# A two-layer attention trunk on one core: the planner takes any two accesses to one PSUM bank, one of them a write, as dependent

## The chip, the cores and the metric

The kernel runs on one core of one Trainium2 chip. The metric is the device time of one execution in microseconds, the median of three runs. All durations further down come from one profiled execution of the kernel before.

## What is computed

Two layers, each a pre-norm mixer over 512 tokens of width 1024. One input projection feeds three causal attention branches; each branch is gated, projected and merged. The change touches the part of branch A, differential attention with four heads of two softmax maps each:

```python
s = jnp.einsum('bqhcd,bkhcd->bhcqk', qb, k) * scale
pr = masked_softmax(s, kpos[None, :] <= tpos[:, None])
a = pr[:, :, 0] - lam * pr[:, :, 1]
o = jnp.einsum('bhqk,bkhe->bqhe', a, v)          # 4 heads, 128 wide
...
o = rmsnorm(o, subln_g) * (1.0 - lam_init)
branches = jnp.stack([o_a * silu(a_g), o_b * silu(b_g), o_c * silu(c_g)], axis=2)
x = x + jnp.sum(sigmoid(merge) * (branches @ w_up), axis=2) @ w_out
```

Around it stand the projections of the other branches, which are computed in three products of split operands (high by high, low by high, high by low), so that TensorE carries three matmuls of 512 columns for each 128 by 128 block of weights.

## The kernel before, in words

The program first records every operation in a `Plan` (`add`, line 272), with the tiles that it reads and writes. `Plan.put_down` (line 387) then goes through the recorded operations with a table of costs and sets, for each of the five engines, the order in which they are written into the program; operations that may run on two engines (weight splits on ACT or POOL, subtractions and sums on POOL or DVE) get their engine there too. Dependences of the reckoning come from `View.box` (line 152), a rectangle of partitions and columns: two accesses depend on each other where their rectangles meet (`meet`, line 329). The program that comes out of it gets its semaphores from the framework below, by what it was told in that order.

In PSUM the program holds two rings of tiles, three of `mm` for the projections and five of `at` for scores, transposes and attention outputs. Each tile is 128 partitions by 512 columns of f32 and is one bank.

`attend_a(h)` (line 1085) is one head of branch A: scores and exponentials of the two maps, the difference of the maps into `P`, and then, as a tail that is woven into other work, `weigh_a` (line 1108). It transposes the four row blocks of `P` into PSUM, copies each to `PTh` on ACT, and multiplies. Products of row block i go to columns 128 i to 128 i + 127 of one bank `po`; block i has i + 1 matmuls, ten for a head. I call the four groups put 0 to put 3. Then ACT reads the bank in four pieces of 128 columns, each divided by its row sum, and squares each piece:

```python
T.matmul(po[:, i * P : (i + 1) * P], at[:, j * P : (j + 1) * P],
         AV[j][:, h * P : (h + 1) * P], start=j == 0, stop=j == i)
...
A.activation(on[:, i * P : (i + 1) * P], po[:, i * P : (i + 1) * P], AF.Copy, scale=rr[:, 0, i : i + 1])
A.activation(junk, on[:, i * P : (i + 1) * P], AF.Square, accum_out=ss[:, i : i + 1])
```

Behind the four reads stand three small DVE instructions and twelve small POOL instructions (an inverse square root, tiles `ss`, `ni`, `rs`, `nt`), four scalings of `on` on ACT, and in `turn` four transposes of `on` on TensorE. In the profile the reads are `o<-at,rr`, the squares `dg<-o`, the scalings `o<-o,rs`, the products `at<-X,PTh`, and the turn's transposes `at<-consts,o`.

Woven around heads 2 and 3 is `c_query` (line 904), which projects a query of branch C, multiplies it by R on DVE into a tile `t`, and lets TensorE multiply that tile by the compressed keys (`at<-KCb,t`), four matmuls. Its softmax has two small DVE instructions, `cm<-cm,gate` and `cm<-cm,consts`, 128 by 8.

Heads 0 to 3 of layer 0 run from about 140 to 262 us of the span, those of layer 1 from about 820 to 945 us. Everything is recorded by one line of the program, so every instruction of the profile has line 471.

Of the kernel before, what the change touches and what calls it, by code (L numbers as in the profile page):

```python
# [126 lines left out]
class View:  # L127
# [23 lines left out]

    def box(self):

        a, b = int(self.cells[(0,) * self.cells.ndim]), int(self.cells[(-1,) * self.cells.ndim])
        w = self.tile.width
        return a // w, b // w, a % w, b % w
# [62 lines left out]
class Plan:  # L219
# [52 lines left out]
    def add(self, names, call, args, kw):  # L272
# [15 lines left out]
        for x in op.ins:  # L288
            box = x.box()
            for b, w in x.tile.writes:  # L290
                if self.meet(b, box):
                    op.after.add(w)
        for x in op.outs:
            box, t = x.box(), x.tile
            for line in (t.writes, t.reads):
                for b, w in line:
                    if self.meet(b, box):
                        op.after.add(w)
# [1231 lines left out]
```

## Time and profile before

| | |
|---|---|
| three runs | 1411.82, 1410.4, 1412.04 us; median 1411.82 |
| the profiled execution | 1409.82 us, its span 1408.0 us |
| mean granted clock of TensorE | 0.996 of full |
| TensorE busy | 1378.9 us, 98% of the span, 6882 matmuls |
| VectorE busy | 1046.4 us, 74% |
| ScalarE busy | 790.3 us, 56% |
| GpSimd busy | 567.3 us, 40% |
| TensorE without work, all gaps | about 29 us |

Busy time of matmuls runs to a modelled end, so successive matmuls overlap by some 0.16 us; what a stop costs is read from start to start. The page's table of slices shows TensorE in its highest tenth all along, and the other engines between.

### The profile page before, as it was taken

The numbers are of one execution on the slowest core, as the hardware profiler recorded it, in microseconds if no ns is written. First come the engines' busy times: TensorE is split into PE (matmuls) and PEld (weight loads), VectorE is DVE, ScalarE is ACT, GpSimd is POOL, SyncE is SP. The second block draws the span as 40 slices with busy tenths as digits, with TensorE's granted clock in tenths as the row PEclk, the third lists the DMA queues.
The fourth block names the chain that finished last, engine by engine and source line by source line (L and its number), as shares of the span: only waits on it lengthen the run. The fifth ranks groups of instructions, "written<-read, shape, count | busy, mean of one in ns | idle before, by whom it ended". The sixth has DMA issues, their size and how long they took to land.

```text
span 1408.0 us, 20777 instructions
## 1 busy us (share of the span) xinstructions
PE 1378.9 (98%) x6882; PEld 1153.3 (82%) x6882; DVE 1046.4 (74%) x2348; ACT 790.3 (56%) x1831; POOL 567.3 (40%) x613
## 2 busy tenths in 40 slices
PE   9999999999999999999999999999999999999997
PEld 7888877888888888888887888778888888888886
DVE  7688888888887566555785888897888855666566
ACT  6455655866764356334444656567677734643443
POOL 3464466545343152122251744774445322313040
PEclk9999999999999999999999999999999999999998
DMA  6223221111222221342422231312112222124221
GB/s 246 98 83 101 72 89 62 61 61 53 75 68 83 85 88 61 106 149 98 147 83 97 83 98 52 106 55 67 60 61 68 76 83 89 62 75 157 97 91 68
DMA packets 67932, 123.65 MB, mean 88 GB/s; under 512 B 7920, under 2 KB 10224, under 8 KB 67824
## 3 DMA queue, kind: packets, MB, share of 16 engines
q1 hardware_dynamic: 62640, 113.14, 24.5%
q10 hardware_dynamic: 5184, 9.18, 1.9%
q8 instruction: 54, 0.88, 0.2%
q14 instruction: 54, 0.44, 0.1%
HBM read 117.57 MB, written 4.72 MB: 87 GB/s over the span
## 4 chain that ended last, share of the span: by engine, by line
PE 89%; DVE 5%; ACT 1%; issue 1%; POOL 0%; DMA 0%; DVEq 0%; POOLq 0%; ACTq 0%; SPq 0%
PE mm L471 70%; PE at L471 19%; DVE t L471 1%; DVE nt L471 0%; DVE P L471 0%; POOL nt L471 0%; DVE cm L471 0%; DMA raw<-W 0%; DVE K L471 0%; DVE rstd L471 0%; ACT o L471 0%; DVE g L471 0%; DVE wlo L471 0%; DVE x L471 0%; DVE hr L471 0%
## 5 line engine op out<-in xcount | busy, mean ns | idle before, releaser
L471 PE MATMUL mm<-HI,whi 128*128 128x512 f32 x1240 | 496.9, 401 | 2.1 <-POOL whi L471 1.1
L471 PE MATMUL mm<-HI,wlo 128*128 128x512 f32 x1240 | 488.7, 394 | 1.6 <-DVE wlo L471 1.0
L471 PE MATMUL mm<-LO,whi 128*128 128x512 f32 x1240 | 488.0, 394 | 1.3 <-DVE LO L471 1.3
L471 POOL TENSOR_SCALAR whi<-raw 128x512 fp32r<-128x512 f32 (+1 forms) x191 | 130.5, 684 | 535.2 <-PE mm L471 357.2
L471 POOL TENSOR_TENSOR wlo<-raw,whi 128x512 fp32r<-128x512 f32 (+1 forms) x191 | 256.9, 1348 | 188.0 <-ACT whi L471 151.6
L471 PEld LDWEIGHTS mm<-HI,wlo 128*128 128x128 f32 x1240 | 233.9, 189 | 51.0 <-DVE wlo L471 1.4
L471 PEld LDWEIGHTS mm<-HI,whi 128*128 128x128 f32 x1240 | 234.3, 189 | 41.8 <-POOL whi L471 1.6
L471 ACT CAST whi<-raw 128x512 fp32r<-128x512 f32 (+1 forms) x205 | 125.2, 614 | 254.8 <-PE mm L471 185.5
L471 PEld LDWEIGHTS mm<-LO,whi 128*128 128x128 f32 x1240 | 234.4, 189 | 40.0 <-DVE LO L471 2.3
L471 DVE TENSOR_TENSOR wlo<-raw,whi 128x512 fp32r<-128x512 f32 (+1 forms) x205 | 149.7, 735 | 79.6 <-ACT whi L471 43.9
L471 ACT ACTIVATE P<-P,mx 128x512 f32<-128x512 f32 (+3 forms) x256 | 142.4, 557 | 65.7 <-DVE mx L471 64.6
L471 PE MATMUL at<-K,Q 128*128 128x256 f32 (+3 forms) x608 | 138.9, 325 | 0.0
L471 PEld LDWEIGHTS at<-K,Q 128*128 128x128 f32 x608 | 103.1, 189 | 16.1 <-issue 0.5
L471 DVE TENSOR_TENSOR t<-mm,R 128x512 f32<-128x512 f32 (+1 forms) x101 | 69.0, 683 | 61.1 <-PE mm L471 57.8
L471 DVE CUSTOM_DVE_ANT_0 P<-at,consts 128x128 f32<-128x128 f32 x208 | 93.8, 470 | 21.6 <-PE at L471 20.5
L471 DVE TENSOR_TENSOR PTl<-at,PTh 128x512 fp32r<-128x512 f32 x192 | 87.0, 484 | 28.2 <-ACT PTh L471 21.6
L471 POOL TENSOR_TENSOR Q<-t,Q 64x512 fp32r<-64x512 f32 x64 | 87.5, 1367 | 34.9 <-ACT Q L471 29.3
L471 PE MATMUL at<-consts,P 128*128 128x128 f32 x560 | 96.1, 272 | 0.8 <-ACT PTh L471 0.7
L471 ACT ACTIVATE P<-P,rc 128x128 f32<-128x128 f32 x192 | 92.0, 552 | 7.9 <-DVE rc L471 6.9
L471 ACT CAST PTh<-at 128x512 fp32r<-128x512 f32 x192 | 74.4, 420 | 38.4 <-PE at L471 31.1
L471 PEld LDWEIGHTS at<-consts,P 128*128 128x128 f32 x560 | 71.5, 140 | 22.1 <-ACT PTh L471 1.3
L471 PE MATMUL mm<-BRh,whi 128*128 128x512 f32 x192 | 77.0, 405 | 0.5 <-DVE t L471 0.5
(222 smaller groups left out, 2126.5 us busy)
## 6 DMA issues: line engine op xcount, KB each, us to landing
raw<-W SPq DMA_DIRECT2D x396, 256.0 KB, 2.6
raw<-WK SPq DMA_DIRECT2D x16, 176.0 KB, 2.3
X<-xT ACTq DMA_DIRECT2D x10, 256.0 KB, 4.1
res<-X ACTq DMA_DIRECT2D x8, 256.0 KB, 2.0
X<-res ACTq DMA_DIRECT2D x8, 256.0 KB, 3.4
out<-K SPq DMA_DIRECT2D x8, 256.0 KB, 2.5
X<-xT SPq DMA_DIRECT2D x6, 256.0 KB, 4.8
P<-xN SPq DMA_DIRECT2D x3, 512.0 KB, 6.0
```

The lines of the kernel that those rows point to most:

```text
L471: getattr(getattr(self.nc, op.engine), call)(*real, **kw)
```

## The change

A view of a PSUM tile now has the whole tile as its rectangle. For the recorded dependences this means: a read of some columns depends on the last write to the bank that was recorded before it, whatever its columns; a write depends on every read and write of that bank recorded before it.

```diff
     def box(self):
 
+        if self.tile.space == "psum":
+            return 0, self.tile.shape[0] - 1, 0, self.tile.width - 1
         a, b = int(self.cells[(0,) * self.cells.ndim]), int(self.cells[(-1,) * self.cells.ndim])
         w = self.tile.width
         return a // w, b // w, a % w, b % w
```

Of the 11,239 recorded operations 24 get an operation to wait for that they had not waited for, directly or through others on the same engine: the first three reads `o<-at,rr` of each of the eight heads (four heads, two layers). They waited for put 0, 1 and 2, and now wait for the last matmul of put 3. All else in the program is the same, but the order of the five engines is worked out anew. It differs from the first of these reads on to shortly behind the fourth head, in either layer; ahead of that, between the layers and behind, the instructions stand as before, and the DMA queue of SP is the same throughout. In the two stretches some 300 of 6673 TensorE instructions, 200 of DVE's, 100 of ACT's and 60 of POOL's stand elsewhere. 22 two-input operations (weight remainders `wlo`, rotary sums) go from POOL to DVE and 16 the other way; ACT gets two casts more than it gives.

The first place is ACT at head 0 of layer 0. `o_420` is the head's output, `at_385` its PSUM bank, `dg` the square; the wait is by semaphore, named after the engine waited for. Before:

```order
L471 ACTIVATE o_420_1657<-at_385_1648,rr_342_1375 128x128 [waits PE_49]
L471 ACTIVATE K_395_1663<-t_393_1641 64x512 [waits DVE_49]
L471 ACTIVATE K_395_1663<-t_393_1641 64x512
L471 ACTIVATE K_397_1678<-t_393_1641 64x512 x2
L471 ACTIVATE dg_421_1689,ss_386_1690<-o_420_1657 128x128 [waits Activation_49]
L471 ACTIVATE o_420_1657<-at_385_1648,rr_342_1375 128x128 [waits PE_49]
L471 ACTIVATE dg_422_1699,ss_386_1690<-o_420_1657 128x128 [waits Activation_49]
L471 ACTIVATE o_420_1657<-at_385_1648,rr_342_1375 128x128
L471 ACTIVATE dg_423_1713,ss_386_1690<-o_420_1657 128x128 [waits Activation_49]
L471 ACTIVATE t_409_1724<-t_408_1715 128x512 [waits DVE_49]
L471 ACTIVATE o_420_1657<-at_385_1648,rr_342_1375 128x128 [waits PE_49]
L471 ACTIVATE dg_424_1737,ss_386_1690<-o_420_1657 128x128 [waits Activation_49]
```

After:

```order
L473 CAST whi_446_1702<-raw_445_1595 128x512 [waits DMAHW1_49,PE_49,Pool_49]
L473 ACTIVATE t_409_1714<-t_408_1706 128x512 [waits DVE_49]
L473 ACTIVATE o_420_1722<-at_385_1648,rr_342_1375 128x128 [waits PE_49]
L473 ACTIVATE dg_421_1729,ss_386_1730<-o_420_1722 128x128 [waits Activation_49]
L473 ACTIVATE o_420_1722<-at_385_1648,rr_342_1375 128x128
L473 ACTIVATE dg_422_1739,ss_386_1730<-o_420_1722 128x128 [waits Activation_49]
L473 ACTIVATE o_420_1722<-at_385_1648,rr_342_1375 128x128
L473 ACTIVATE dg_423_1747,ss_386_1730<-o_420_1722 128x128 [waits Activation_49]
L473 ACTIVATE o_420_1722<-at_385_1648,rr_342_1375 128x128
L473 ACTIVATE dg_424_1769,ss_386_1730<-o_420_1722 128x128 [waits Activation_49]
```

The four reads, which stood between other work and each waited for its put, now stand together behind the casts and the key halves `K`, and only the first of them waits for TensorE.

The second place is TensorE at the same head, between put 0 and put 2 (`X` is a tile of values, `PTh` a transposed block; `mm_405` is a projection that is woven in). Before:

```order
L471 MATMUL mm_405_1628<-LO_32_153,whi_400_1556 128x512
L471 MATMUL mm_405_1628<-HI_31_144,wlo_401_1561 128x512
L471 MATMUL at_385_1648<-X_142_810,PTh_390_1528 128x128
L471 MATMUL at_385_1648<-X_143_819,PTh_390_1528 128x128 [waits Activation_49]
L471 MATMUL mm_405_1628<-HI_33_155,whi_400_1556 128x512
L471 MATMUL mm_405_1628<-LO_34_162,whi_400_1556 128x512
```

After:

```order
L473 MATMUL mm_405_1628<-LO_32_153,whi_400_1556 128x512
L473 MATMUL mm_405_1628<-HI_31_144,wlo_401_1561 128x512
L473 MATMUL at_385_1648<-X_142_810,PTh_390_1528 128x128
L473 MATMUL at_385_1648<-X_143_819,PTh_390_1528 128x128
L473 MATMUL mm_405_1628<-HI_33_155,whi_400_1556 128x512
L473 MATMUL mm_405_1628<-LO_34_162,whi_400_1556 128x512
```

The instructions are the same ones. Before, the second matmul of put 1, which writes columns 128 to 255, waits for ACT, which by then has the read of columns 0 to 127 in its queue; now it waits for nothing.

The third place is DVE ahead of the second `c_query` product of layer 0, whose operand is `t_644`. `mm_638` is its projection, `acc_92` the top-k scores of branch B, `P_549` the difference of the softmax maps of head 3, `cm_601` the factors of the first `c_query`. Before:

```order
L471 TENSOR_TENSOR t_629_2535<-mm_608_2390,R_76_403 128x512 [waits PE_49]
L471 MATCH_REPLACE acc_92_633<-m8_567_2352,acc_92_633 128x384
L471 RECIPROCAL rr_642_2265<-st_618_2455 128x4 [waits Activation_49]
L471 TENSOR_TENSOR cm_601_2444<-cm_601_2444,gate_44_594 128x8 [waits DVE_49]
L471 MAX m8_625_2556<-acc_92_633 128x8
L471 TENSOR_TENSOR cm_601_2444<-cm_601_2444,consts_3_185 128x8 [waits DVE_49]
L471 TENSOR_TENSOR t_644_2570<-mm_638_2503,R_76_403 128x512 [waits PE_49]
L471 STREAM_SHUFFLE t_646_2577<-mm_638_2503 128x512 [waits Pool_49]
```

After:

```order
L473 TENSOR_SCALAR ni_615_2543<-ss_569_2424 128x4 [waits DVE_49]
L473 TENSOR_SCALAR rs_614_2546<-ni_615_2543 128x4 [waits DVE_49]
L473 TENSOR_TENSOR cf_643_2549<-st_550_2163,rr_642_2300 128x4
L473 SCALAR_TENSOR_TENSOR g_631_2555<-t_630_2540,t_629_2532 128x512 [waits Activation_49]
L473 TENSOR_SCALAR cf_643_2549<-cf_643_2549,nlam_90_405 128x4 [waits DVE_49]
L473 SCALAR_TENSOR_TENSOR P_549_2149<-P_617_2469,cf_643_2549,P_549_2149 128x128 [waits DVE_49]
L473 SCALAR_TENSOR_TENSOR P_549_2149<-P_617_2469,cf_643_2549,P_549_2149 128x256
L473 SCALAR_TENSOR_TENSOR P_549_2149<-P_617_2469,cf_643_2549,P_549_2149 128x384
L473 SCALAR_TENSOR_TENSOR P_549_2149<-P_617_2469,cf_643_2549,P_549_2149 128x512
L473 TENSOR_TENSOR t_644_2590<-mm_638_2512,R_76_403 128x512 [waits PE_49]
L473 STREAM_SHUFFLE t_646_2605<-mm_638_2512 128x512
```

The two small `cm_601` instructions, which stood one and three places ahead of `t_644`, now stand seventeen and eighteen places ahead of it. In their place stand the four differences of head 3 and three small instructions of head 2 (`ss`, `ni`, `rs`). On TensorE, the product with `KCb` came six matmuls of 512 columns behind the last of `mm_638`; now three of them and nine transposes of `P_549` stand there.

## Rows read from the trace of the kernel before

**Rows 1.** the page: busy time of each engine, and the chain that ended last

```profile
PE 1378.9 (98%) x6882; PEld 1153.3 (82%) x6882; DVE 1046.4 (74%) x2348; ACT 790.3 (56%) x1831; POOL 567.3 (40%) x613
...
PE 89%; DVE 5%; ACT 1%; issue 1%; POOL 0%; DMA 0%; DVEq 0%; POOLq 0%; ACTq 0%; SPq 0%
```

**Rows 2.** stretches; columns: busy per engine (instructions), granted clock, DMA share, GB/s

```profile
200.00:262.00 62.00, 58.93 (x301) 47.77 (x300) 54.49 (x126) 37.78 (x103) 43.97 (x58) 0.97 0.20 67
...
880.00:945.00 65.00, 61.84 (x327) 50.82 (x327) 57.64 (x141) 39.45 (x110) 48.62 (x69) 1.00 0.27 86
```

**Rows 3.** PE's waits over the span: for whom, us in total, times, longest

```profile
PE at L471 <- ACT o L471: 4.0, 8, 0.6
```

**Rows 4.** timeline, head 0: start, length, engine, operation [idle before <-whom]

```profile
148.52 0.38 PE L471 MATMUL at<-X,PTh 128*128 128x128 f32 x2
...
148.94 0.37 ACT L471 ACTIVATE o<-at,rr 128x128 f32<-128x128 f32 x1 [0.28 <-PE at L471]
...
149.36 0.49 PE L471 MATMUL at<-X,PTh 128*128 128x128 f32 x2 [0.46 <-ACT o L471]
...
153.83 1.05 PE L471 MATMUL at<-X,PTh 128*128 128x128 f32 x8
```

**Rows 5.** timeline, head 2: a short hold, then the last long one

```profile
210.87 0.60 PE L471 MATMUL at<-consts,P 128*128 128x128 f32 x4
...
211.49 0.71 PE L471 MATMUL at<-X,PTh 128*128 128x128 f32 x4
...
905.38 0.71 PE L471 MATMUL at<-X,PTh 128*128 128x128 f32 x4 [0.46 <-ACT o L471]
```

**Rows 6.** timeline: ACT's reads of head 0, its scaling, and head 1's first turn

```profile
152.11 0.34 ACT L471 ACTIVATE o<-at,rr 128x128 f32<-128x128 f32 x1
...
152.79 0.35 ACT L471 ACTIVATE o<-at,rr 128x128 f32<-128x128 f32 x1
...
155.68 0.31 ACT L471 ACTIVATE dg<-o 128x128 f32<-128x128 f32 x1
...
160.64 1.28 ACT L471 ACTIVATE o<-o,rs 128x128 f32<-128x128 f32 x4 [1.20 <-POOL rs L471]
...
189.70 0.33 PE L471 MATMUL at<-consts,o 128*128 128x128 f32 x1 [0.62 <-ACT o L471]
```

**Rows 7.** timeline: ahead of the second product with KCb, both layers

```profile
227.87 2.52 POOL L471 TENSOR_TENSOR wlo<-raw,whi 128x512 fp32r<-128x512 f32 x2
...
228.11 1.09 DVE L471 TENSOR_TENSOR cm<-cm,gate 128x8 f32<-128x8 f32 x1
...
229.72 0.69 DVE L471 TENSOR_TENSOR cm<-cm,consts 128x8 f32<-128x8 f32 x1
...
231.07 1.10 PE L471 MATMUL at<-KCb,t 128*128 128x64 f32 x8 [1.59 <-DVE t L471]
...
922.87 1.10 PE L471 MATMUL at<-KCb,t 128*128 128x64 f32 x8 [1.60 <-DVE t L471]
```

**Rows 8.** tile cm: duration in ns, min/median/max, first and last start

```profile
L471 DVE TENSOR_TENSOR cm<-cm,gate x8: 172/174/1103, 228.1 to 1023.9; 128x8 f32<-128x8 f32 x8
...
L471 DVE TENSOR_TENSOR cm<-cm,consts x8: 166/168/692, 229.7 to 1024.1; 128x8 f32<-128x8 f32 x8
```

**Rows 9.** one stretch right behind 231.07, columns as in rows 2

```profile
232.00:236.00 4.00, 4.00 (x13) 3.14 (x13) 3.90 (x11) 1.67 (x3) 3.56 (x6) 0.57 0.10 37
```

**Rows 10.** timeline of PE: the wait for one weight remainder

```profile
191.96 0.40 PE L471 MATMUL mm<-HI,whi 128*128 128x512 f32 x1
...
192.19 0.40 PE L471 MATMUL mm<-LO,whi 128*128 128x512 f32 x1
...
193.57 0.50 PE L471 MATMUL mm<-HI,wlo 128*128 128x512 f32 x1 [0.98 <-DVE wlo L471]
```

**Rows 11.** tile wlo, 140 to 262 us: duration in ns, min/median/max

```profile
L471 POOL TENSOR_TENSOR wlo<-raw,whi x18: 1264/1292/1742, 141.3 to 258.7; 128x512 fp32r<-128x512 f32 x18
...
L471 DVE TENSOR_TENSOR wlo<-raw,whi x11: 682/685/1121, 143.7 to 240.6; 128x512 fp32r<-128x512 f32 x11
```


## The prediction

> **What bounds the kernel now.** I read the page first: TensorE is busy for 1378.9 of 1408.0 us, and 89% of the chain that ended last is its own work [rows 1]. The change adds and takes away no matmul, so time can only come from where TensorE stops, some 29 us in all, and from its clock. The new order differs from the old one only around the four heads of branch A in either layer, so I looked there next: in the stretch 200 to 262 us TensorE is without work for 3.1 us and DVE is busy for 54.5 of 62, in 880 to 945 us for 57.6 of 65 [rows 2]. TensorE is the bound, and DVE stands close behind it. Then I asked whom TensorE waits for: the longest entry over the whole span is ACT's tile `o`, 8 times, 4.0 us [rows 3]. The timeline shows what that is. In head 0 the first matmul of put 1 starts at 148.52, ACT reads the columns of put 0 from 148.94 to 149.31, and only at 149.36 does TensorE go on with the next matmul, which writes other columns of that bank [rows 4]. Its semaphore names ACT. So on the chip the program already takes the bank as one, and the plan, which did not know it, put the read between two writes.
>
> **What the reads cost now.** Eight matmul passes of put 3 take 1.05 us, of which the last is 0.27 long, so a pass comes every 0.11 us and a matmul, two passes, every 0.22. The held one comes 0.84 us after the one before it, a loss of 0.62 [rows 4]. There are six like it: put 1 of heads 0 and 1, put 3 of head 2, in both layers, the first at 149.36 and the last at 905.38, each with 0.46 us idle [rows 4, 5]. They make 2.8 of the 4.0 us; the other two entries, 0.62 and 0.61, are of another kind, below. Six more are short: four transposes from 210.87 in 0.60 us, the last of them starting about 211.20, and the held matmul at 211.49 where 0.11 later was possible, a loss of 0.18 [rows 5]. That is 6 x 0.62 + 6 x 0.19 = **4.9 us**. In the new order every one of the 24 reads stands behind the last matmul of its put 3, in all eight heads, so all of this goes. Nothing hides it now: TensorE's other work stands behind the held matmul in the same queue. What is late next is ACT's chain to the turn.
>
> **What the later reads cost.** Three reads and three squares that were done early now follow put 3. Back to back, reads come every 0.68 us (152.11, 152.79), so the last square starts about 2.5 us after put 3, and from the last square to the end of the first scaling it is 155.68 to 160.64 + 0.40, or 5.4 [rows 6]. That makes 7.8 us from put 3 to a possible turn, where it was 6.2. In the new order TensorE has 44, 55, 76 and 67 instructions of other work between put 3 and the turn of heads 0 to 3, from start to start, at 0.23 us for a matmul of 512 columns [rows 10], 0.11 for a transpose or a pass [rows 4, 5] and so on, 9.4, 11.4, 15.6 and 12.8 us; before, head 1 had 27 in 5.5 us and waited for 0.62 [rows 6]. So the wait of head 1, 0.79 start to start in each layer, may go, and head 0 has 1.6 us left for whatever DVE and POOL have queued ahead of the small instructions. Bounds: 1.6 us gained, or a wait as long as head 1's at two more heads in each layer, 3.2 lost. I take **0**.
>
> **The second product with KCb.** It is TensorE's longest stop: 1.59 us in layer 0, 1.60 in layer 1 [rows 7], and right behind the first of them the clock was granted at 0.57 over 4 us [rows 9], which is the lower level, 1.2 GHz, for most of it, at a cost of 4 x 0.43 = 1.7 us. Behind the second stop, which is as long, the granted clock stays at 1.00 [rows 2]. The operand `t` on DVE is late because two instructions of 128 by 8 ahead of it took 1.09 and 0.69 us; their usual time is 0.17 [rows 7, 8], so the excess is 1.45 us. Both end when one of POOL's two subtractions, 227.87 to 230.39, ends [rows 7]. In the new order the two stand seventeen places earlier, where more slack lies behind them, and in front of the operand stand small POOL steps of 0.2 us. Bounds: nothing gained if the delay is handed down the queue, or 1.6 a layer. I take the excess as gone, **2.9 us**, and with so short a stop the slow stretch too, **1.7 us**.
>
> The Trainium skill ("SBUF — State Buffer", Who interferes with whom) says that DVE and GpSimd share one port pair as an exclusive lock, against a DVE instruction with two SBUF inputs, and that the loser waits for the whole instruction. The trace agrees: an instruction of 0.17 us lasts until POOL's ends. By that rule the 1.45 us belong to the overlap, not to the place, and can come back wherever a POOL subtraction runs; kept in full it would make the sum 4.6 us worse, which is the first rival below.
>
> **Smaller ones.** In layer 0 alone TensorE waits for a remainder `wlo`, 1.38 us between the starts at 192.19 and 193.57 where 0.23 is usual (191.96 to 192.19): 1.15 [rows 10]. That subtraction goes to POOL, which takes 1.29 us for one where DVE takes 0.69 [rows 11], but starts earlier in the queue. Between 0 and 1.15, I take half, **0.6 us** gained. DVE gets six instructions more than it loses, at 0.69 us each 4.1 us [rows 11], in stretches where it is 88% busy [rows 2]; between all and none of it delays TensorE, I take half, **2.1 us** lost. The two casts more on ACT lie beside other work: ACT is busy for 38 of 62 us [rows 2].
>
> **Sum.** The profiled execution took 1409.8 us. 4.9 + 2.9 + 1.7 + 0.6 - 2.1 = 8.0 us off, 1401.8. The three runs have a median 2.0 above that execution, so I expect 1403.8. That is 0.57% faster.
>
> **The rivals.** *The delay goes along.* The two small instructions meet a POOL subtraction at their new place too, or DVE carries its lateness down the queue to `t`. Then the 2.9 and 1.7 stay: 1411.8 - 3.4 = 1408.4. For it: DVE's queue is in order and 88% full. Against: between the two and `t` there are now waits of DVE for TensorE and ACT, which take up lateness.
>
> *Given back.* TensorE comes earlier to everything, and waits there for DVE and ACT, which have their own work to do: what the bank costs now is hidden by what comes after it. For it: DVE has only 7.5 us to spare in 62, and the stop at KCb is DVE's. Against: the reads cost TensorE directly, and DVE has some to spare. Of the 4.9 us one would be left: 1410.8, no change.
>
> *Slower.* The 22 operations that go to DVE meet POOL's at its port and take the 1.12 us that the longest there took; the 16 that leave save 0.69 each [rows 11]. That is 24.6 - 11.0 = 13.6 us more on an engine whose queue is in order, and if it all ends up in TensorE's waits, 13.6 - 4.9 = 8.7 slower: 1420.5. It decides from the point at which more than 5 of the 13.6 land on TensorE. Against it: most instructions on DVE there take the usual 0.69.
>
> *It does not do what it says*, if some other read keeps a bank from TensorE: 1411.8. The order shows none in these heads.
>
> **How the numbers follow.** Forecast 1403.8, chance 0.48; the delay goes along, 1408.4, 0.22; given back, 1410.8, 0.20; slower, 1420.5, 0.08; not what it says, 0.02. A measurement of this kernel can tell about 0.2%, 2.8 us: faster means below 1409.0, slower above 1414.6. Of the second case most lies below 1409.0. Faster 0.66, same 0.26, slower 0.08. The low end is all bounds at their best: 4.9 + 1.6 + 3.2 + 1.7 + 1.15 = 12.5 off, 1399.3. The high end, 1411.2, takes in the first rival and most of the second and leaves out what is slower.
>
> **What would show it.** In the profile after, TensorE's waits for ACT's `o` should have no `at<-X,PTh` among them, and successive puts should come every 0.22 us: if not, the first term is wrong. The product with KCb should stop for less than 0.5 us with a full clock behind it; the small `cm` instructions should take 0.17 us or lie where they do no harm. At the turns a wait of over 0.6 us in head 0 would show that the later reads do cost. DVE busy for over 93% of the second half of the heads, with TensorE waiting for its tiles, would be the second or third rival.

## The result, and the profile after

The changed kernel takes **1396.9 us** (median of 4 runs, 1395.4 to 1398.3) against 1411.1 for the kernel before, a ratio of 0.990 with a 95% interval of 0.988 to 0.992. The forecast was 1403.8 with a range from 1399.3 to 1411.2: the direction was right, and the time is 6.9 us lower than forecast, below the whole range.

The page after, busy time of each engine and the chain that ended last, against [rows 1]:

```profile
PE 1372.8 (98%) x6882; PEld 1150.3 (82%) x6882; DVE 1039.9 (75%) x2354; ACT 790.9 (57%) x1833; POOL 559.0 (40%) x605
...
PE 90%; DVE 3%; POOL 1%; ACT 1%; issue 1%; DMA 0%; DVEq 0%; POOLq 0%; ACTq 0%
```

DVE has six instructions more and is busy for 6.5 us less. That is the first surprise. The stretches of the heads, columns as in [rows 2]:

```profile
200.00:262.00 62.00, 61.85 (x339) 52.00 (x339) 57.32 (x145) 45.05 (x123) 42.45 (x59) 1.00 0.22 70
...
880.00:945.00 65.00, 64.87 (x354) 54.45 (x354) 59.85 (x150) 47.08 (x130) 44.11 (x59) 1.00 0.24 74
```

In the same 62 us TensorE has 339 matmuls, some of them smaller ones, instead of 301, its idle time has fallen from 3.1 to 0.15 us, and the clock is full. DVE is now busy for 92% of either stretch, and TensorE has no wait of over 0.15 us for it there. Whom TensorE waits for over the whole span, against [rows 3]:

```profile
PE mm L473 <- DVE LO L473: 2.2, 4, 1.3
PE mm L473 <- POOL whi L473: 1.7, 2, 0.9
PE mm L473 <- DVE VW L473: 1.3, 1, 1.3
PE at L473 <- ACT o L473: 1.2, 2, 0.6
```

The eight waits for ACT's `o` are two; the first three lines lie outside the heads. The timeline of the places that the prediction spoke of: head 0's puts and reads, head 1's turn, the second product with KCb.

```profile
148.06 0.38 PE L473 MATMUL at<-X,PTh 128*128 128x128 f32 x2
148.98 0.61 PE L473 MATMUL at<-X,PTh 128*128 128x128 f32 x4
...
155.03 0.35 ACT L473 ACTIVATE o<-at,rr 128x128 f32<-128x128 f32 x1
...
157.10 0.35 ACT L473 ACTIVATE o<-at,rr 128x128 f32<-128x128 f32 x1
...
194.76 0.33 PE L473 MATMUL at<-consts,o 128*128 128x128 f32 x1 [0.58 <-ACT o L473]
...
225.28 0.82 PE L473 MATMUL at<-consts,P 128*128 128x128 f32 x6
225.93 1.00 PE L473 MATMUL at<-KCb,t 128*128 128x64 f32 x8
```

The four passes of put 1 run as one group of 0.61 us (in [rows 4] two of them came 0.84 us after the first two). The four reads stand together behind put 3. Of the turns that of head 1 still waits, and that of head 3 a little. The product with KCb follows the transposes at once; in [rows 7] it came after 1.59 us without work.

Where the time went: TensorE runs the same 572 instructions from the start of put 0 of head 0 to a place shortly behind head 3, in another order. That stretch takes 118.9 instead of 127.2 us in layer 0 and 119.1 instead of 124.4 in layer 1, together 13.65 less; all the rest of the program is equal to within half a microsecond. A stop is the distance from start to start beyond the usual one. The stops in the stretch, in us:

| stop of TensorE | before, layer 0 / 1 | after, layer 0 / 1 |
|---|---|---|
| bank holds, six a layer | 2.45 / 2.45 | 0 / 0 |
| turn of head 1 | 0.79 / 0.78 | 0.74 / 0.79 |
| turn of head 3 | 0 / 0 | 0.31 / 0.30 |
| `wlo` | 1.15 / 0 | 0 / 0 |
| `hr` (a small product, operand copied by DVE) | 0.61 / 0.58 | 0 / 0 |
| the two products with KCb | 1.75 / 1.77 | 0.23 / 0.23 |
| slow clock behind it | 1.6 / 0 | 0 / 0 |
| `mm<-BRh,whi`, waits for DVE's `t` | 0.42 / 0.41 | 0 / 0 |
| `at<-PTl,VS`, waits for DVE's `PTl` | 0.40 / 0.38 | 0 / 0 |

Three of these stops stand in no row so far; in layer 0 of the kernel before:

```profile
219.89 0.43 PE L471 MATMUL mm<-small,hr 128*128 128x64 f32 x2 [0.44 <-DVE hr L471]
...
258.28 0.47 PE L471 MATMUL mm<-BRh,whi 128*128 128x512 f32 x1 [0.25 <-DVE t L471]
...
261.76 0.50 PE L471 MATMUL at<-PTl,VS 128*128 128x512 f32 x1 [0.24 <-DVE PTl L471]
```

### The profile page after: what moved, and what is told of

It is laid out like the page before. It is cut to its first block, busy times and chain, and to the rows that moved or that the text cites. A ratio compares the mean times of both kernels' runs of the same rounds, so it can differ in the third digit from the quotient of the medians.

```text
span 1394.4 us, 20787 instructions
## 1 busy us (share of the span) xinstructions
PE 1372.8 (98%) x6882; PEld 1150.3 (82%) x6882; DVE 1039.9 (75%) x2354; ACT 790.9 (57%) x1833; POOL 559.0 (40%) x605
## 4 chain that ended last, share of the span: by engine, by line
PE 90%; DVE 3%; POOL 1%; ACT 1%; issue 1%; DMA 0%; DVEq 0%; POOLq 0%; ACTq 0%
PE mm L473 71%; PE at L473 19%; POOL nt L473 1%; DVE t L473 0%; DVE nt L473 0%; DVE P L473 0%; DMA raw<-W 0%; POOL rs L473 0%; DVE rstd L473 0%; DVE pc L473 0%; POOL whi L473 0%; DVE BV L473 0%; DVE cm L473 0%; ACT t L473 0%; DVE g L473 0%
## 5 line engine op out<-in xcount | busy, mean ns | idle before, releaser
L473 POOL TENSOR_TENSOR wlo<-raw,whi 128x512 fp32r<-128x512 f32 (+1 forms) x195 | 262.2, 1348 | 195.2 <-ACT whi L473 147.4
L473 DVE TENSOR_TENSOR wlo<-raw,whi 128x512 fp32r<-128x512 f32 (+1 forms) x201 | 146.3, 732 | 83.0 <-ACT whi L473 47.8
```

The costliest lines, as they stand in the source:

```text
L473: getattr(getattr(self.nc, op.engine), call)(*real, **kw)
```

## The experiments

Two theories at first. Theory 1: the bank holds cost what they cost directly, 4.9 us, and the other 8.8 come from the rest of the new order. Theory 2: the holds make TensorE late, so that DVE and POOL meet where the plan had them apart, and the other stops follow from the holds.

### The reads alone moved, in the old order

```diff
+HEADS = (1217, 1468, 1758, 1914, 6744, 6995, 7285, 7441)
...
+        for s in HEADS:
+            last = self.ops[s + 6]
+            for k in range(6):
+                self.ops[s + k].start = last.start - 0.001 * (6 - k)
         E = mybir.EngineType
```

The numbers are those of the first read `o<-at,rr` of each head among the recorded operations; three reads and three squares follow each other there.

> The order of before on all engines but ACT; there the first three reads and squares of each of the eight heads are written directly ahead of the fourth read, behind put 3. Nothing else is planned anew. Theory 1 (the bank holds cost 4.9 us and no more; the rest of the 13.7 us that the profiled executions differ by comes from the new order of DVE and POOL): TensorE's waits for tile o between puts go, the stops at hr (219.9), KCb (231.1), BRh with t (258.3) and PTl (261.8) stay, and head 1's turn waits 1 to 1.6 us longer in each layer, since the old order has only 27 instructions there: 1411.1 - 4.9 + 2 to 3.2, so 1408 to 1409.5. Theory 2 (the holds make TensorE late, and by that DVE and POOL meet where the plan had them apart): the later stops go too, 1411.1 - 13.7 + 2 to 3.2, so 1399.5 to 1400.6.

Measured: 1412.9, ratio to before 1.001 (1.000 to 1.002). No gain at all. TensorE's stops in the timeline, layer 0 and one of layer 1:

```profile
165.66 1.21 PE L478 MATMUL at<-consts,o 128*128 128x128 f32 x4 [0.55 <-ACT o L478]
...
194.46 0.33 PE L478 MATMUL at<-consts,o 128*128 128x128 f32 x1 [2.24 <-ACT o L478]
...
234.28 1.10 PE L478 MATMUL at<-KCb,t 128*128 128x64 f32 x8 [1.61 <-DVE t L478]
...
927.45 1.10 PE L478 MATMUL at<-KCb,t 128*128 128x64 f32 x8 [1.61 <-DVE t L478]
```

The holds are gone, and the turns take their place: head 1's loses 2.41 us where it lost 0.79, and head 0's, which had not waited, 1.3 over its four transposes. A wait of 0.64 for ACT's `o` comes at a score matmul of either layer, and the clock is low behind the stop at KCb in both. It is low behind head 1's turn too, four microseconds in each layer, columns as in [rows 2], which costs some 1.6 us a time:

```profile
195.00:199.00 4.00, 4.00 (x16) 3.43 (x16) 2.61 (x7) 2.33 (x9) 2.58 (x4) 0.61 0.00 0
888.30:892.30 4.00, 4.00 (x16) 3.49 (x17) 2.47 (x7) 2.33 (x9) 2.54 (x4) 0.66 0.00 0
```

The stop at KCb itself is 1.77, with holds or without. Those at BRh and PTl stay. `hr` and `wlo` have no stop here, though the order of DVE and POOL is that of before; no copy of `hr` takes over 0.62 us in this run, where one took 1.28. So theory 2 falls for the larger stops, and theory 1 was too hopeful: the reads can only stand late if the turns are moved back too, and in the old order they aren't.

### The reads alone moved back, in the new order

```diff
+AHEAD = {1217: (1168, 1178, 1178),
+         1468: (1428, 1429, 1438),
...
+        for s, puts in AHEAD.items():
+            for i, p in enumerate(puts):
+                for k in (0, 1):
+                    op = self.ops[s + 2 * i + k]
+                    op.start = min(op.start, self.ops[p].start + 0.05 + 0.6 * k)
         E = mybir.EngineType
```

> The order of after on all engines but ACT; there the first three reads and squares of each head are moved ahead again, each to the place behind the same matmul of its bank that it had in before. Theory 1 (the holds cost 4.9 us and no more): three long and three short waits for tile o in each layer are back, 1396.9 + 4.9 = 1401.8, or up to 1.5 less if the turn of head 1 waits less; hr, KCb, BRh with t and PTl stay without a stop. Theory 2 (holds make TensorE late, so that DVE and POOL meet): most of 13.7 us is lost again, about 1408 to 1410.5.

Measured: 1405.1, ratio to before 0.995 (0.994 to 0.996), by the medians 8.2 above after. The two stretches take 123.3 and 123.5 us, 4.4 more each.

```profile
149.82 0.49 PE L488 MATMUL at<-X,PTh 128*128 128x128 f32 x2 [0.46 <-ACT o L488]
...
213.42 0.71 PE L488 MATMUL at<-X,PTh 128*128 128x128 f32 x4 [0.57 <-ACT o L488]
214.20 1.00 PE L488 MATMUL at<-KCb,t 128*128 128x64 f32 x8
...
228.80 1.00 PE L488 MATMUL at<-KCb,t 128*128 128x64 f32 x8
```

In the new order fewer other matmuls stand between the puts of heads 2 and 3, so all six holds of a layer are long ones: 0.62, 0.62, 0.62, 0.73, 0.59 and 0.62, together 3.8 of the 4.4. Of the rest, 0.33 and 0.30 are the turn of head 2. The stops at `hr`, KCb, BRh and PTl do not come back, though the holds make TensorE late again. This confirms the price of a hold, and that in the new order the other stops do not hang on the holds.

### The two small cm instructions behind t, in the old order

```diff
+        for d in (0, 5527):
+            shuffle = self.ops[1869 + d]
+            for k in (0, 1):
+                self.ops[1740 + d + k].start = shuffle.start + 0.001 * (k + 1)
         E = mybir.EngineType
```

> The order of before on all engines but DVE; there the two small cm instructions of the first c_query (128 by 8, 1.09 and 0.69 us beside POOL's subtractions) are written behind t and the shuffle that the second product with KCb needs, in both layers. Theory 1 (these two held instructions alone make the stop at KCb, and the slow clock behind it in layer 0 comes from that stop): the stop goes from 1.75 to about 0.3 in both layers and the granted clock stays full: 1411.1 - 2.9 - 1.6 = 1406.6. Rival (DVE is late there anyway, or the next instruction with two inputs meets the same POOL subtraction): no change, 1410.4 to 1411.8.

Measured: 1408.9, ratio to before 0.998 (0.997 to 0.999). DVE behind the shuffle, POOL's product beside it, then TensorE:

```profile
230.32 0.52 DVE L475 TENSOR_TENSOR cm<-cm,gate 128x8 f32<-128x8 f32 x1
230.87 1.21 DVE L475 TENSOR_TENSOR cm<-cm,consts 128x8 f32<-128x8 f32 x1
...
230.77 1.29 POOL L475 TENSOR_TENSOR t<-t,sinb 128x512 f32<-128x512 f32 x1
...
229.81 1.10 PE L475 MATMUL at<-KCb,t 128*128 128x64 f32 x8
...
236.02 0.33 PE L475 MATMUL at<-consts,P 128*128 128x128 f32 x1 [0.92 <-DVE P L475]
```

The stop at KCb is gone, and the granted clock behind it is full. But the delay went along: the two instructions take 1.73 us beside the end of a POOL subtraction and the POOL product behind it, where 0.34 is usual and they had taken 1.78. TensorE now waits for DVE's `P` six us later, 1.08 from start to start, and 0.25 at the turn of head 3, in both layers. So of the 1.75 us 1.33 were handed down, and what was won for good is the slow clock of layer 0 and little more. The Trainium skill states ("SBUF — State Buffer", Who interferes with whom) that DVE and GpSimd share a port pair, that whoever issues first has it for the whole instruction, and that the other is blocked. The trace agrees: `cm<-cm,consts` takes 1.21 us and ends with POOL's product.

The run shows one thing more. Up to these instructions its order is that of before, yet `wlo` makes a stop of 0.72 and 0.74 in the two layers, where before has 1.15 and none. It is the same DVE subtraction, which lasts another time (0.68 is usual), as does the instruction ahead of it; layer 0 of before, then of this run:

```profile
192.40 1.12 DVE L471 TENSOR_TENSOR wlo<-raw,whi 128x512 fp32r<-128x512 f32 x1
```

```profile
192.14 1.78 DVE L475 TENSOR_TENSOR wlo<-raw,whi 128x512 fp32r<-128x512 f32 x1
```

So a stop of this kind is not fixed by the order alone: it varies from layer to layer and from run to run.

### Twelve more DVE instructions in the new order

```diff
+TWICE = (1599, 1825, 1838, 2172, 2235, 2290)
...
                 getattr(getattr(self.nc, op.engine), call)(*real, **kw)
+                if op.seq in TWICE or op.seq - 5527 in TWICE:
+                    getattr(getattr(self.nc, op.engine), call)(*real, **kw)
```

> The kernel after with six of DVE's subtractions in the second half of the heads (five wlo, one BRl; 0.68 us each) written twice in each layer, 8.2 us more on DVE in all; the second write gives the same values. Theory of the prediction (half of what is added to DVE delays TensorE): 1396.9 + 4.1 = 1401. Rival A (DVE has room even at 92% busy, since what it does is asked for later): 1396.9 to 1397.7. Rival B (DVE bounds the stretch): 1396.9 + 8.2 = 1405.1.

Measured: 1407.4, ratio to before 0.997 (0.996 to 0.998), 10.5 above after. The stretch and TensorE's longest waits:

```profile
200.00:262.00 62.00, 59.51 (x328) 49.94 (x327) 57.87 (x138) 41.67 (x115) 41.90 (x57) 1.00 0.20 62
```

```profile
PE at L476 <- DVE mx L476: 2.2, 2, 1.1
PE at L476 <- DVE PTl L476: 1.8, 2, 1.2
PE at L476 <- DVE PC L476: 1.5, 2, 0.8
```

DVE is busy for 57.87 of 62 us, hardly more than after, and TensorE stops for what DVE is late with. None of its waits there is for a tile that was written twice (`wlo`, `BRl`): the extra instructions delay what stands behind them in DVE's queue. 4.1 us of DVE work in each layer cost 6.6 and 4.4 us; of the 6.6 some 1.7 are the lower clock (0.57 over 4 us) behind the last of these stops:

```profile
267.50:271.50 4.00, 4.00 (x15) 3.37 (x14) 2.58 (x8) 0.89 (x3) 0.32 (x1) 0.57 0.09 33
```

So rival B was right, and more: with DVE at 92% these twelve found no room, since its spare time isn't where it is wanted.

### Engines swapped, order kept

Theory A was that the choice of engines makes the difference, theory B that the order does. `MOVED` lists the 60 operations for which the two plans choose different engines, by the engine of the other plan.

```diff
+        for engine, line in MOVED.items():
+            for s in line:
+                self.ops[s].engine = engine
         E = mybir.EngineType
```

> The order of before, put down at the same planned starts, but the 60 operations (30 in each layer) for which the new plan chooses another engine run on the engine of after: 22 sums and subtractions from POOL to DVE, 16 the other way, 12 casts from POOL to ACT, 10 the other way. In the profiles so far DVE instructions are held by POOL for 14.9 and 13.9 us in the two stretches of the heads before, for 9.5 and 9.9 after, and that difference is what the stops at wlo, hr, KCb, BRh with t and PTl hang on. Theory A (the choice of engines makes the difference): held time falls to about 10 us a stretch, the stops for DVE go, the six bank holds stay: 1411.8 - 8 = about 1404. Theory B (the order does): held time stays at 14, the stops stay or others take their place: 1410 to 1413.

> The order of after, put down at the same planned starts, but the 60 operations run on the engines that before had chosen for them. Theory A (the choice of engines makes the difference): DVE is held for about 14 us a stretch again, TensorE stops for DVE again, no bank hold: 1397 + 8 = about 1405. Theory B (the order does): held time stays near 10 us, 1397 to 1399.

Measured: the old order with the new engines 1421.0, ratio 1.007 (1.006 to 1.008); the new order with the old engines 1418.3, ratio 1.005 (1.004 to 1.006). Both are slower than either kernel. One stop of each, the second far longer than any stop of before or after:

```profile
232.76 1.10 PE L479 MATMUL at<-KCb,t 128*128 128x64 f32 x8 [1.61 <-DVE t L479]
```

```profile
216.92 1.97 PE L481 MATMUL at<-KCb,t 128*128 128x64 f32 x8 [3.24 <-DVE t L481]
```

I call the time of DVE's instructions beyond the median of their kind (tile and shape) held time, counted where it is over 0.05 us. In before and after all of it lies in instructions that overlap one of POOL's. Counted so it is 14.8 and 13.8 us in the two stretches of before and 10.6 and 10.8 in those of after (9.5 and 9.9 in the expectation are a little low). In the old order with the new engines it is only 8.4 a stretch, and yet all the old stops but that at `wlo` are there and some more. Neither theory holds. The sum of held time is no measure; what counts is which instruction is held, and whether TensorE asks for its result in that time. The planned starts were worked out for the other choice of engines, so that either run also breaks a plan: how much order and engines are worth each by itself can't be read from them.

### The same small changes of the plan, with the rule and without

If order and engines go together, one order may be lucky. So the plan was shaken by one number, in both kernels alike.

```diff
-            return (0.2 if n < 64 else 0.065 + 0.0024 * n), 0.1
+            return (0.28 if n < 64 else 0.065 + 0.0024 * n), 0.1
...
-        return (0.2 if n < 64 else 0.12 + 0.00098 * n), 0.1
+        return (0.28 if n < 64 else 0.12 + 0.00098 * n), 0.1
```

That is the change of `pool_028` and `before_028`. The other pair has, in both places of the costs of DVE and ACT:

```diff
-            return us, 0.06
+            return us, 0.1
```

> The kernel after with one number of the plan changed: a POOL instruction of under 64 columns is reckoned at 0.28 us, which is the distance from start to start in the trace, and not at 0.20, so that the twelve small POOL steps ahead of each turn end 1 us later in the plan. All orders are worked out anew. If the turn of head 1 (0.74 and 0.79 us) and that of head 3 (0.31 and 0.30) are late only by these steps, they go: 1396.9 - 2 = 1395. If the new order meets more of POOL on DVE's port, it is slower: by what DVE is held longer, us for us, since the run with twelve more DVE instructions showed no room there; up to 1405.

> The kernel after, unchanged, beside the others of this call, so that they can be compared with it on one chip: 1396 to 1398.

> The kernel before with one number of the plan changed, the same as in pool_028: a POOL instruction of under 64 columns at 0.28 us instead of 0.20. Reads and writes of other columns of a bank are independent as before, but the orders are worked out anew (700 of 6673 TensorE instructions and most of DVE's in the heads stand elsewhere). Theory 1 (the rule on the bank is what the 13.7 us come from, in any order that the plan makes): bank holds and stops for DVE of about the same size as in before, 1409 to 1413. Theory 2 (4.9 us come from the bank holds, the rest is the draw of one order against another): the stops for DVE are others and smaller, 1402 to 1406.

> The kernel before with another number of the plan changed: what is reckoned between the end of an instruction on DVE or ACT and the start of one on another engine that waits for it, 0.10 us instead of 0.06. Theory 1 (the rule on the bank, in any order): 1409 to 1413. Theory 2 (the draw of one order against another, beside 4.9 us for the holds): anywhere between 1402 and 1415.

> The kernel after with the same number changed as in before_lag. Theory 1 (the rule on the bank, in any order): 1396 to 1399, some 13 us below before_lag. Theory 2 (the draw): stops for DVE that after happens not to have come back, up to 1406; the distance to before_lag is then anything from 5 us up.

Measured, with the stretches of the heads (the same 572 instructions of TensorE in each) from the traces:

| plan | without the rule: us (layer 0 / 1) | with it: us (layer 0 / 1) |
|---|---|---|
| as it was | 1411.1 (127.2 / 124.4) | 1396.9, again 1397.0 (118.9 / 119.1) |
| small POOL steps at 0.28 | 1405.8 (122.9 / 122.9) | 1397.2 (118.8 / 120.5) |
| 0.10 between engines | 1417.7 (126.1 / 125.2) | 1402.6 (118.4 / 119.2) |

The third plan loses 7 to 9 us ahead of the heads, with the rule and without. With the rule the heads take 118.4 to 120.5, without it 122.9 to 127.2. But the size depends on the draw: less the bank holds of each plan (2.45, 2.8 and 1.5 us a layer) the rule is worth from -0.3 to 6.2 us a layer. `before_028` has its bank holds, 2.8 us a layer, and none of the stops at `hr`, KCb, BRh and PTl; it has one at a weight remainder instead:

```profile
179.17 0.49 PE L471 MATMUL at<-X,PTh 128*128 128x128 f32 x2 [0.46 <-ACT o L471]
...
194.61 0.50 PE L471 MATMUL mm<-HI,wlo 128*128 128x512 f32 x1 [1.61 <-POOL wlo L471]
```

`before_lag`, again another order, has `hr` and KCb once more, 0.73 and 1.60. And `pool_028`, which did away with the wait of head 1's turn (0.20 of 0.74 is left), got 0.80 for DVE's `P` in exchange:

```profile
229.50 0.63 PE L473 MATMUL at<-consts,P 128*128 128x128 f32 x4 [0.64 <-DVE P L473]
```

In its layer 1 a stop of 0.76 at `hr` is back, with the rule in force. It is as fast as after, not faster.

### The rule for one half of the heads

```diff
-        if self.tile.space == "psum":
+        if self.tile.space == "psum" and self.tile.name in BANKS:
```

> The rule on the whole bank for the output banks of heads 0 and 1 alone; for all other banks of PSUM two accesses meet by their columns, as before. The order up to head 2 is that of after, from there on it is a new one, with the reads of heads 2 and 3 between their puts. Theory 1 (what goes, goes where the order is new; each half of the heads by itself): the two long holds of heads 0 and 1 go in each layer and the stop at wlo, 2.5 + 1.2; the second half keeps some 1 us of holds a layer and gets stops for DVE by the draw: 1397 + 2 to 1397 + 8, with holds only in heads 2 and 3. Theory 2 (the stops of the second half, hr, KCb, BRh with t and PTl, hang on the reads of heads 2 and 3): 1411.8 - 3.7, about 1408, with the stops of before.

> The rule on the whole bank for the output banks of heads 2 and 3 alone. Up to head 2 the order is that of before: two long holds and the turn of head 1 in each layer, wlo in layer 0. Theory 1 (each half by itself): these 2.5 + 1.2 us stay, the holds of heads 2 and 3 go, and the stops of the second half are those of a new order: 1411.8 - 2 = 1410 if hr, KCb, BRh with t and PTl stay in place, down to 1402 if they go. Theory 2 (the stops of the second half hang on the reads of heads 2 and 3): they go, 1402. Theory 3 (they hang on the holds and reads of heads 0 and 1): they stay, 1410.

Measured: heads 0 and 1 alone 1398.6, ratio to before 0.991 (0.990 to 0.992); heads 2 and 3 alone 1401.3, ratio 0.993 (0.992 to 0.995). The gains, 12.3 and 9.6 against the kernel before measured beside them, add up to far more than the 14.2 that the medians give for the whole rule. With the rule for heads 0 and 1 alone the reads of heads 2 and 3 stand between their puts, and one long hold is there, but the products with `hr` and with KCb have no stop:

```profile
203.15 0.33 PE L476 MATMUL mm<-small,hr 128*128 128x64 f32 x2
...
210.53 0.94 PE L476 MATMUL at<-X,PTh 128*128 128x128 f32 x6 [0.46 <-ACT o L476]
...
211.30 1.00 PE L476 MATMUL at<-KCb,t 128*128 128x64 f32 x8
```

With the rule for heads 2 and 3 alone the holds of heads 0 and 1 and the wait for `wlo` stand as they were, and `hr`, BRh and PTl have no stop; of that at KCb 0.27 is left in layer 0 and 0.93 in layer 1:

```profile
177.65 0.49 PE L476 MATMUL at<-X,PTh 128*128 128x128 f32 x2 [0.46 <-ACT o L476]
...
217.41 0.33 PE L476 MATMUL mm<-small,hr 128*128 128x64 f32 x2
227.00 1.08 PE L476 MATMUL at<-KCb,t 128*128 128x64 f32 x8
```

So these stops hang neither on the reads of heads 2 and 3 nor on those of heads 0 and 1. The other orders of the second half lost them in part or whole: `before_028` has none of them, `before_lag` kept `hr` and KCb, `pool_028` has `hr` in one layer.

## Why the prediction was wrong

| step | forecast, us | measured, us |
|---|---|---|
| bank holds | -4.9 | -4.9 |
| later reads, at the turns | 0 | +0.6 |
| the products with KCb | -2.9 | -3.1 |
| slow clock | -1.7 | -1.6 |
| `wlo` | -0.6 | -1.2 |
| six more DVE instructions | +2.1 | 0, no stop that is theirs |
| `hr`, BRh with `t`, PTl | not counted | -2.8 |
| many under 0.2 each | not counted | -0.7 |
| sum | -8.0 | -13.7 |

The remaining 1.3 us of the miss lie in the last step: the profiled execution of before was 2.0 below the median of its three runs, that of after only 0.7 below its median.

**The bank holds** were right in mechanism and size, and the experiment that put them back measured 0.62 for a long one again. **The later reads**, taken as 0, cost 0.6 net; the reason given, more instructions between put 3 and the turn, is the right one, since without them, in the old order, they cost all that the holds had cost.

Two steps failed. **The first put stops at nothing without a reason**: `hr`, BRh with `t` and PTl were in the trace of before, at 0.4 to 0.6 us each, below the entries that I priced, and stood in the stretches whose order was worked out anew. They went, 2.8 us together. This is the step that put the time below the range: its low end, 1399.3, already had DVE's term at nothing, and with 2.8 more it would have been 1396.5, just under the 1396.9 measured. The one at `hr` is of the same kind as that at KCb, a copy of 128 by 31 that takes 0.17 us as a rule, held until POOL's subtraction ends, here in the timeline of the kernel before:

```profile
218.51 1.29 POOL L471 TENSOR_TENSOR wlo<-raw,whi 128x512 fp32r<-128x512 f32 x1
...
218.55 1.28 DVE L471 COPY hr<-x 128x31 f32<-128x31 f32 x1
```

It has one input, so looking for held instructions among those with two inputs alone would miss it. The hold itself has not gone. After, one of the four copies is held for 1.27 us in either layer; but they are done at 202.35, and TensorE asks for them 1.1 us later:

```profile
200.82 1.53 DVE L473 COPY hr<-x 128x31 f32<-128x31 f32 x4
```

```profile
203.47 0.33 PE L473 MATMUL mm<-small,hr 128*128 128x64 f32 x2
```

So what the new order changed there is the distance between the held instruction and its reader.

**The second is the step of DVE**, +2.1 for six more instructions. Half of their time was too low a price (twelve of them, put in by hand, cost more than their whole time), and the item was wrong. Over the span, DVE's instructions at their median times make 4.6 us more work, as the count says, but the time beyond the medians is 9.9 us less, 7.2 of it in the two stretches; so DVE is busy for 6.5 us less, and TensorE has no stop that is due to the six. Counting instructions on an engine whose durations depend on its neighbour gave the wrong sign.

**KCb** came out near the number. After, `cm<-cm,gate` is still held at its earlier place, for 0.59 and 0.50 us, nine us ahead of the product, and harmlessly: the slack behind it, which the prediction named, is there. That the earlier place alone did it is not shown: no run moved the two instructions ahead in the old order, and behind `t` they handed 1.33 of 1.75 us on. **The slow clock** went with the stop, as forecast, there and in the run that removed the stop alone; that it was there to be won in layer 0 and not in layer 1 no run explains. Part of the 1.2 us at `wlo` is luck in the same way, since that stop changed between runs of one order.

Of the rivals, "the delay goes along" is what the old order does, and "given back" is what the late reads do there; neither is what the new plan does. "Slower" had its price right, us for us on DVE, and its amount wrong.

What is shown: 4.9 us are the bank holds; the other 8.8 are stops that this one order of the kernel before had and that other orders without the rule had only in part. What stays open is whether the rule does more than remove the holds: with it the heads were 2.5 to 8.3 us a layer shorter in all three settings of the plan, but less the holds nothing was left in one layer, and three settings are few.

## What to carry to other kernels

When a change makes a scheduler work out a stretch anew, price the direct effect from the trace, and then treat every stop in that stretch, small ones too, as open: it can go or be exchanged for another, so that the range must reach to all of them gone. Before crediting or blaming the rule, shake the scheduler by an unrelated number with the old rule and with the new; here that alone moved the old kernel 7 us down and 5 up. And an engine that is 90% busy, and whose instructions last longer beside another engine's, is priced neither by its count of instructions nor by its busy time (the old order with the new engines has 4.6 us less of it than after and is 24 us slower): ask which instruction the bound engine waits for, and how long before that it is done.

## What the runs showed of the chip

A stop of the same length is followed by the lower clock at one time and not at another. Behind the KCb stop of 1.6 us idle, four microseconds each, columns as in [rows 2]; first the old order with late reads, layer 0 and layer 1, then the old order with the new engines, both layers:

```profile
235.00:239.00 4.00, 4.00 (x14) 3.20 (x14) 3.89 (x11) 1.63 (x3) 3.59 (x5) 0.58 0.16 53
928.00:932.00 4.00, 4.00 (x14) 3.21 (x14) 3.90 (x12) 1.24 (x3) 3.53 (x5) 0.57 0.17 57
```

```profile
233.50:237.50 4.00, 4.00 (x21) 3.35 (x21) 3.89 (x13) 1.24 (x2) 1.83 (x4) 1.00 0.15 50
929.50:933.50 4.00, 4.00 (x20) 3.35 (x20) 3.90 (x13) 1.24 (x2) 1.91 (x4) 1.00 0.17 59
```

In the kernel before it was 0.57 in layer 0 and full in layer 1 [rows 2, 9], and so it was in `before_lag`, behind 1.44 and 1.45 us idle. Longer stops don't settle it: 2.24 and 2.23 us idle at head 1's turn with late reads were followed by 0.61 and 0.66, but 2.20 and 2.18 us idle at a score matmul of the old order with the new engines by the full clock. A slow stretch costs about 1.6 us, and what decides it isn't settled by these runs.
